# Operand addresses, retention operands one pair at a time, and later weight sums in a four-layer decoder trunk

## The chip, the cores and the metric

The kernel runs as one program on one core of one Trainium2 chip. The metric is device time in microseconds, from launch to end, as the median of three runs. TensorE does the matrix products (its sequencer loads weights and streams a moving operand past them), VectorE (DVE) and ScalarE (ACT) do the elementwise work, GpSimd (POOL) and SyncE (SP) mostly issue DMAs. SBUF is the on-chip memory: 128 partitions, each with one row of bytes in which every tile has a start address. PSUM is where TensorE leaves sums.

## What is computed

Four sub-layers on 512 tokens of width 1024, each with an RMSNorm ahead and a residual add behind: retention, gated FFN, stick-breaking attention, gated FFN; then a last RMSNorm.

```python
for i in range(DEPTH):            # DEPTH = 2
    x = x + _retention(_rmsnorm(x, ret_norm[j]), ...)         # i = 0
    x = x + _stick_breaking(_rmsnorm(x, sb_norm[j]), ...)     # i = 1
    x = x + _conv_ffn(_rmsnorm(x, ffn_norm[i]), ...)          # both
return _rmsnorm(x, final_norm)
# _retention: proj = h @ w_in (q, k, v, g of 4 heads), rotary, chunked decay attention,
#             y = silu(g) * normed o; y @ w_out
# _conv_ffn:  u = h @ w_up; depthwise conv of width 3; (silu(gate) * val) @ w_down
```

All of it is float32. The kernel forms each float32 product from rounded parts: an operand is split into `hi` and `lo`, and a product is hi*hi + hi*lo + lo*hi, three matmuls.

## The kernel before

**Loads.** Every weight chunk goes through `chunk` (L154): SP issues a DMA into a `raw` buffer, ACT casts it to `hi`, DVE subtracts to get `lo` (L159, L160). The buffers are rings of 4 while retention runs and 5 afterwards. A chunk of 1024 columns serves 24 matmuls of 512 columns, or 24 of 256.

**Products.** `mm3` (L163 to L168) and the loops at L357 and L646 issue the three matmuls. In most products the weights are `hi`/`lo` and the moving operand is an activation: `xh`/`xl` (the normed input of a sub-layer), `yy`/`qk` (retention's output), `oh`/`ol` (FFN), `oo` (stick-breaking). For the values of retention and stick-breaking it is the other way: `xh`/`xl` or `xo` are the weights and `hi`/`lo` move.

**Seven products instead of eight.** `seven` (L294) computes a 2x2 block product with seven block products: for retention's heads 2 and 3 (tensors fqk, fv, fg) and for two stages of each FFN's down-projection (fast0_0, fast0_1, fast1_0, fast1_1). It needs sums of weight blocks, which `weight_sums` (L372) makes in DRAM with accumulating DMAs on POOL's queue, in the order of `ORDER`, and sums of operand blocks, which for retention `ret_operands` (L436) makes into `xo` tiles on DVE and ACT, for pairs of k tiles: pairs 0 and 1 in one call, pairs 2 and 3 in another.

**Order in retention** (L516). Head 0; then q, k, v of head 1; operands of pairs 0 and 1; `out_proj(steps, 2)`, half of head 0's output projection (each piece is one weight chunk, 24 matmuls and two adds into `x` at L220); scores, values and gate of head 1; then the pool of the normed input is given back and `xb` takes its place; operands of pairs 2 and 3; the other half of head 0's output projection; all four pieces of head 1's; then heads 2 and 3 by seven products. A planner in the framework may move an instruction ahead of another on its engine where nothing forbids it, so an engine's queue is only roughly in program order. An output projection's sums lie in `acc`, of which there are three.

**Addresses.** SBUF tiles lie on two stacks in every partition's row, and each tile starts at a multiple of 32 bytes. On the left stack stand constants (`vec`, `x`, `ones`, `diag`, ...) up to byte 21,824, which is 64 past a multiple of 256, and then `raw`, `hi`, `lo`, `tt` and the tiles of a phase. All of their sizes, with one exception, are multiples of 256 (the `sg` tiles of stick-breaking are not, but together they take 10,496 bytes, 41 x 256), so every matrix operand there starts 64 past a multiple of 256: `hi`, `lo`, `oh`, `ol`, `yy`, `qk`, `oo` and others. The right stack holds `xh`, `xl`, `xo`, `vx` and grows down from byte 229,344, which is 224 past a multiple of 256; so all of these start 224 past one. A matmul takes slices at multiples of 256 bytes within a tile, which leaves the remainders as they are. The small exceptions are `ones` (160 past) and the identity (0).

Of the kernel before, what the change touches and what calls it, by code (L numbers as in the profile page):

```python
# [9 lines left out]
F32 = mybir.dt.float32  # L10
# [5 lines left out]
P = 128  # L16
D = 1024
S = 512
KD = D // P
# [9 lines left out]
FAST = (2, 2)  # L29
TAIL = 18  # L30
Q = S // 2
HALF = S // 2

ORDER = (
    ("fqk", 0, 1), ("fv", 0, 2), ("fg", 0, 1), ("fqk", 1, 1), ("fg", 1, 1), *((f"fast{l}_{s}", 0, 2) for l in range(2) for s in range(FAST[l])),
)
SUMS = {n for n, _, _ in ORDER}
WARM = 4
RAW = 4
FAST_HEAD = 2  # L40
# [3 lines left out]
class Kernel:  # L44
# [12 lines left out]
    def __init__(self, ctx, tc, t):  # L57
        self.tc, self.nc, self.t = tc, tc.nc, t
        self.const = ctx.enter_context(tc.tile_pool(name="const", bufs=1))
        self.wp = ctx.enter_context(tc.tile_pool(name="wp", bufs=1))  # L60
        self.ap = ctx.enter_context(tc.tile_pool(name="ap", bufs=1))
        self.dp = ctx.enter_context(tc.tile_pool(name="dp", bufs=1, space=bass.MemoryType.DRAM))
        self.ps = ctx.enter_context(tc.tile_pool(name="ps", bufs=1, space=bass.MemoryType.PSUM))
        self.n = 0
        self.pp, self.xpools = None, []
        self.tiles = dict.fromkeys(("raw", "hi", "lo"), 0)
        self.att_pool()
        self.phase("ret")
        self.operands("xa", "xs")
# [130 lines left out]
    def out_proj(self, name, base, ys, last):  # L200
        for _ in self.out_proj_steps(name, base, ys, last):
            pass
# [167 lines left out]
        x, z = ([self.att() for _ in range(2)] for _ in range(2))  # L370
        self.seven(name, i, product, add, x, z, n)

    def weight_sums(self):


        nc, tc, t = self.nc, self.tc, self.t
        self.sums = {n: {} for n in SUMS}
        gate = nc.gpsimd.tensor_copy(self.gate, self.x[KD - 1][:, :1])
        with tc.issue_after(getattr(gate, "ins", gate)):
            for name, first, n in ORDER:  # L380
                w, cs = t[name], range(first, first + n)
                cols = w.shape[3]
                d = {
                    c: [
                        self.dp.tile([P, cols + 16], F32, tag=f"{name}_{c}_{i}", bufs=1, name=self.name("sum"))[:, :cols]
                        for i in range(4)
                    ]
                    for c in cs
                }
                self.sums[name].update(d)  # L390
                s = lambda c, i: d[c][i]
                for to, of in ((0, 2), (2, 0), (0, 3), (2, 2), (1, -1), (1, 0), (3, -2), (3, 1)):
                    for c in cs:
                        if (to, of) in ((0, 3), (2, 2), (1, 0), (3, 1)):
                            nc.gpsimd.dma_start(s(c, to), w[c][of], accum_op=ALU.add)
                        else:
                            nc.gpsimd.dma_start(s(c, to), w[c][of] if of >= 0 else s(c, -1 - of))
# [136 lines left out]
    def retention(self):  # L534
        nc, t = self.nc, self.t
        first = self.first4("rfirst", load=True)
        self.xpl = [self.xa, None]

        def angles(r):
            self.cos, self.sin = self.sb("tr"), self.sb("tr")  # L540
            nc.sync.dma_start(self.cos, t["cos"])
            nc.sync.dma_start(self.sin, t["sin"])
            if r is not None:
                nc.vector.tensor_mul(self.cos, self.cos, r)
                nc.vector.tensor_mul(self.sin, self.sin, r)

        def out_proj(steps, n):
            for _ in range(8 * n):
                next(steps, None)

        def out_steps(h, y, last=None):
            return self.out_proj_steps("rout", 4 * h, y, last)

        angles(self.r)
        nc.sync.dma_start(self.vec[:, 5 * KD :], t["vec"][:, 5 * KD :])
        self.rc = self.token_major_r()
        self.weight_sums()
        self.ops = []
        qk = self.ret_qk(0, first)
        v = self.ret_v(0)  # L560
        y = self.ret_y(0, self.ret_av(v, self.ret_scores(0, *qk)))
        qk = self.ret_qk(1, [])
        v = self.ret_v(1)
        self.ret_operands((0, 1))
        steps = out_steps(0, y)
        out_proj(steps, 2)
        y = self.ret_y(1, self.ret_av(v, self.ret_scores(1, *qk)))

        self.less_operands()
        self.more_operands("xb")  # L570
        self.xpl[1] = self.xp
        angles(None)
        self.ret_operands((2, 3))
        out_proj(steps, 2)
        steps = out_steps(1, y)
        out_proj(steps, 4)
        qk = self.ret_qk(2, self.feature_tiles("fqk", 0))
        v = [[self.sb(tag) for tag in tags] for tags in (("yy",) * NT, ("vr", "vr", "vx", "vx"))]
        self.token_rows("fv", 0, 2, S, v)
        y = self.ret_y(2, self.ret_av(self.ret_split(v[0]), self.ret_scores(2, *qk)))  # L580
        qk = self.ret_qk(3, self.feature_tiles("fqk", 1))
        steps = out_steps(2, y)
        out_proj(steps, 2)
        y = self.ret_y(3, self.ret_av(self.ret_split(v[1]), self.ret_scores(3, *qk)))
        out_proj(steps, 2)
        self.operands("xs")
        for _ in out_steps(3, y, 1):
            pass
# [72 lines left out]
    def ffn(self, l, last):  # L661
        a, s = [], 0
        first = self.first4(f"ufirst{l}")
        self.phase("ffn")
        for f in range(NF):
            a.append(self.ffn_act(l, f, first[2 * f : 2 * f + 2] if f < 2 else (None, None)))
            if f == 1:
                self.swap_pool()
            if s < 2 and f == STAGES[l][s][1] + 1:
                lo, hi = STAGES[l][s]  # L670
                for half in range(2):
                    self.fast_down(l, s, a[lo + 1 : hi : 2], half)
                s += 1
        self.swap_pool()
        self.down(l, a, s, last)
        if last is not None:
            self.phase("sb")
        return a
# [336 lines left out]
```

## Time and profile before

| | |
|---|---|
| median of 3 runs | 1392.52 us (1391.12 to 1393.06) |
| the profiled execution | 1390.32 us |
| its span, first to last instruction | 1388.5 us |
| TensorE busy in it | 1365.5 us, 7280 matmuls |
| VectorE, ScalarE, GpSimd busy | 1038.8, 643.4, 111.0 us |
| chain that ended last, share of TensorE | 88% |
| granted TensorE clock, mean | 0.995 |

The profiled execution has 1.8 us around its span and lies 2.2 us below the median of the runs. A matmul's duration in the profile overlaps that of the next one, so what a matmul costs is the spacing from one start to the next; durations of two groups of the same shape can still be compared.

### The profile page before, as it was taken

The page shows a single profiled execution, that of the slowest core. Times are in us where ns is not written, and L with a number is a line of the kernel's source. Part 1 is how long each engine was busy: PE and PEld are TensorE (multiplying, and loading weights), DVE is VectorE, ACT ScalarE, POOL GpSimd, SP SyncE. Part 2 cuts the span into 40 slices and gives each one's busy share as a digit, 9 for nine tenths or more (in the row PEclk, how much of TensorE's full clock was granted, in tenths as well). Part 3 has the DMA queues.
Part 4 walks back from the last instruction along what each step waited for, and adds up shares of the span by engine and source line. Part 5 has one row for each costly group of instructions (what it writes and reads, how often), then busy time and mean ns, then how long its engine had stood idle before and what let it go on. Part 6 is the DMA issues. An engine that isn't in the chain of part 4 may idle for free.

```text
span 1388.5 us, 18974 instructions
## 1 busy us (share of the span) xinstructions
PE 1365.5 (98%) x7280; PEld 1155.5 (83%) x7280; DVE 1038.8 (75%) x1464; ACT 643.4 (46%) x932; POOL 111.0 (8%) x190
## 2 busy tenths in 40 slices
PE   9999989999999999999999999999999999999997
PEld 7888879789988889888988898787778899888887
DVE  7777667678778878688666668879799886787665
ACT  5544435465645444344334454444265443444434
POOL 1222222120000000000000021111000000000000
PEclk9999999999999999999999999999999999999999
DMA  9999999997334325323521564444143345235121
GB/s 323 292 287 266 277 294 322 318 316 213 113 96 140 106 91 168 121 91 105 181 80 40 170 183 125 129 117 105 44 138 94 104 127 162 75 110 173 54 69 62
DMA packets 68107, 217.98 MB, mean 157 GB/s; under 512 B 8112, under 2 KB 10288, under 8 KB 68016
## 3 DMA queue, kind: packets, MB, share of 16 engines
q1 hardware_dynamic: 45760, 146.21, 32.5%
q0 software_dynamic: 20736, 69.22, 19.9%
q10 hardware_dynamic: 1520, 1.33, 0.3%
q8 instruction: 58, 0.95, 0.3%
q14 instruction: 33, 0.27, 0.1%
HBM read 202.05 MB, written 58.72 MB: 188 GB/s over the span
## 4 chain that ended last, share of the span: by engine, by line
PE 88%; DVE 7%; DMA 3%; ACT 1%; issue 1%; DVEq 0%; ACTq 0%; SPq 0%
PE acc L166 19%; PE acc L168 19%; PE acc L167 19%; PE x L646 6%; PE att L166 4%; PE att L167 4%; PE att L168 4%; PE z L646 3%; PE att L646 3%; PE acc L646 2%; PE one L768 1%; PE z L740 1%; DVE sg L745 1%; PE tp L760 1%; DVE lo L160 1%
## 5 line engine op out<-in xcount | busy, mean ns | idle before, releaser
L159 ACT CAST hi<-raw 128x1024 fp32r<-128x1024 f32 (+2 forms) x255 | 247.4, 971 | 383.9 <-PE acc L167 221.8
L160 DVE TENSOR_TENSOR lo<-raw,hi 128x1024 fp32r<-128x1024 f32 (+2 forms) x255 | 285.6, 1122 | 75.8 <-ACT hi L159 74.6
L167 PE MATMUL acc<-xl,hi 128*128 128x512 f32 x704 | 279.2, 397 | 0.0
L168 PE MATMUL acc<-xh,lo 128*128 128x512 f32 x704 | 279.2, 397 | 0.0
L166 PE MATMUL acc<-xh,hi 128*128 128x512 f32 x704 | 279.1, 396 | 0.0
L168 PEld LDWEIGHTS acc<-xh,lo 128*128 128x128 f32 x704 | 132.6, 188 | 32.1
L167 PEld LDWEIGHTS acc<-xl,hi 128*128 128x128 f32 x704 | 132.6, 188 | 31.1 <-issue 0.2
L166 PEld LDWEIGHTS acc<-xh,hi 128*128 128x128 f32 x704 | 132.6, 188 | 30.8
L601 DVE SCALAR_TENSOR_TENSOR tt<-tt,vec,tt 128x511 f32<-128x511 f32 (+1 forms) x176 | 131.4, 748 | 4.3 <-ACT tt L599 1.7
L598 DVE TENSOR_TENSOR tt<-acc,rr 128x512 f32<-128x512 f32 x80 | 55.1, 689 | 86.3 <-PE acc L168 86.0
L220 DVE TENSOR_TENSOR x<-x,acc 128x512 f32<-128x512 f32 x72 | 48.7, 684 | 40.4 <-PE acc L168 40.1
L599 ACT ACTIVATE tt<-tt,vec 128x512 f32<-128x512 f32 x88 | 71.5, 814 | 10.2 <-DVE tt L598 9.0
L646 PE MATMUL att<-xo,hi 128*128 128x256 f32 x384 | 69.4, 282 | 0.0
L646 PEld LDWEIGHTS att<-xo,hi 128*128 128x128 f32 x384 | 59.2, 189 | 0.2
L745 DVE TENSOR_TENSOR_SCAN sg<-sg,diag 128x512 f32<-128x512 f32 (+3 forms) x64 | 52.4, 819 | 2.4 <-ACT sg L742 1.7
L646 PE MATMUL att<-xo,lo 128*128 128x256 f32 x192 | 53.9, 281 | 0.0
L646 PE MATMUL x<-oh,hi 128*128 128x256 f32 x188 | 53.5, 285 | 0.0
L646 PE MATMUL x<-oh,lo 128*128 128x256 f32 x188 | 53.2, 283 | 0.0
L646 PE MATMUL x<-ol,hi 128*128 128x256 f32 x188 | 53.2, 283 | 0.0
L168 PE MATMUL acc<-hi,xl 128*128 128x256 f32 (+1 forms) x160 | 52.5, 328 | 0.0
L167 PE MATMUL acc<-lo,xh 128*128 128x256 f32 (+1 forms) x160 | 52.3, 327 | 0.0
L166 PE MATMUL acc<-hi,xh 128*128 128x256 f32 (+1 forms) x160 | 52.2, 326 | 0.0
(555 smaller groups left out, 3042.6 us busy)
## 6 DMA issues: line engine op xcount, KB each, us to landing
raw<-in_up SPq DMA_DIRECT2D x80, 512.0 KB, 3.6
raw<-sum SPq DMA_DIRECT2D x48, 512.0 KB, 4.2
sum<-in_fast POOLq DMA_DIRECT2D x36, 512.0 KB, 9.7
sum<-sum POOLq DMA_DIRECT2D x24, 512.0 KB, 7.9
raw<-in_fast SPq DMA_DIRECT2D x18, 512.0 KB, 3.6
raw<-in_rout SPq DMA_DIRECT2D x16, 512.0 KB, 6.1
sk<-hl POOLq DMA_DIRECT2D x32, 256.0 KB, 4.4
sum<-in_fqk POOLq DMA_DIRECT2D x12, 512.0 KB, 9.9
```

Source lines behind the costliest of these rows:

```text
L159: nc.scalar.copy(hi, raw)
L160: nc.vector.tensor_sub(lo, raw, hi.bitcast(F32))
L166: mm(out, a[0], b[0], start=start, stop=False)
L167: mm(out, a[0], b[1], start=False, stop=False)
L168: mm(out, a[1], b[0], start=False, stop=stop)
L220: self.nc.vector.tensor_add(self.x[m], self.x[m], ps)
L598: nc.vector.tensor_mul(u, ps, self.r)
L599: nc.scalar.activation(c, u, AF.Identity, scale=w[2], bias=w[3])
L601: nc.vector.scalar_tensor_tensor(c[:, i:], u[:, : S - i], w[2 - i], c[:, i:], op0=ALU.mult, op1=ALU.add)
L646: mm(out[:, :Q], a[ai], b[bi], start=start and k + i == 0, stop=k == nk - 1 and i == 2, skip_group_check=not start)
L740: nc.tensor.matmul(z[:, :nz], q[:, i * P : (i + 1) * P], k[:, :nz], start=m == 0, stop=m == 1)
L745: nc.vector.tensor_tensor_scan(sg[:, :n][:, ::-1], sg[:, :n][:, ::-1], self.diag[:, S - n :][:, ::-1], 0.0, op0=ALU.mult, op1=ALU.max,)
```

## The change

Three things. Two unused tiles of 192 and 224 bytes are laid at the bottom of the left stack and at the top of the right one, so that left and right operands alike start at multiples of 256 bytes (`ones` then lies 96 past one and the identity 192). Retention's second half of operands is made one pair at a time, with a piece of an output projection ahead, between and behind; for that, one piece of head 0's output projection moves from ahead of head 1's scores to behind its gate, and two of head 1's pieces go ahead of head 0's last two. The sums of the second FFN's weights are issued in a call of their own, in the first FFN, behind a read of that FFN's norm factor `r`; before, they were issued with the others, behind the load of the last `x` tile.

```diff
 ORDER = (
-    ("fqk", 0, 1), ("fv", 0, 2), ("fg", 0, 1), ("fqk", 1, 1), ("fg", 1, 1), *((f"fast{l}_{s}", 0, 2) for l in range(2) for s in range(FAST[l])),
+    (("fqk", 0, 1), ("fv", 0, 2), ("fg", 0, 1), ("fqk", 1, 1), ("fg", 1, 1), ("fast0_0", 0, 2), ("fast0_1", 0, 2)),
+    (("fast1_0", 0, 2), ("fast1_1", 0, 2)),
 )
...
         self.const = ctx.enter_context(tc.tile_pool(name="const", bufs=1))
+
+        self.const.tile([P, 48], F32, name="left")
+        right = ctx.enter_context(tc.tile_pool(name="right", bufs=1, side="right"))
+        right.tile([P, 56], F32, name="right")
...
-    def weight_sums(self):
+    def weight_sums(self, order, behind):
...
-        gate = nc.gpsimd.tensor_copy(self.gate, self.x[KD - 1][:, :1])
+        gate = nc.gpsimd.tensor_copy(self.gate, behind[:, :1])
         with tc.issue_after(getattr(gate, "ins", gate)):
-            for name, first, n in ORDER:
+            for name, first, n in order:
...
-        self.weight_sums()
+        self.sums = {}
+        self.weight_sums(ORDER[0], self.x[KD - 1])
...
         steps = out_steps(0, y)
-        out_proj(steps, 2)
+        out_proj(steps, 1)
         y = self.ret_y(1, self.ret_av(v, self.ret_scores(1, *qk)))
...
-        self.ret_operands((2, 3))
+        out_proj(steps, 1)
+        more = out_steps(1, y)
+        for j in (2, 3):
+            self.ret_operands((j,))
+            out_proj(more, 1)
         out_proj(steps, 2)
-        steps = out_steps(1, y)
-        out_proj(steps, 4)
+        out_proj(more, 2)
...
         first = self.first4(f"ufirst{l}")
+        if l == 0:
+            self.weight_sums(ORDER[1], self.r)
         self.phase("ffn")
```

## Rows read from the trace of the kernel before

**Rows 1.** The page, part 1: busy us (share of the span) xinstructions.
```profile
PE 1365.5 (98%) x7280; PEld 1155.5 (83%) x7280; DVE 1038.8 (75%) x1464; ACT 643.4 (46%) x932; POOL 111.0 (8%) x190
```

**Rows 2.** Waits of TensorE: total us, times, longest us.
```profile
PE acc L166 <- DVE x L220: 4.4, 2, 4.0
PE tp L760 <- DVE bt L749: 2.6, 8, 0.6
PE att L166 <- ACT p L490: 2.1, 1, 2.1
PE att L357 <- DVE vx L368: 1.7, 1, 1.7
```

**Rows 3.** TensorE groups by form: out<-moving,weights (any order) xcount | busy us, mean ns.
```profile
L167 PE MATMUL acc<-xl,hi 128*128 128x512 f32 x704 | 279.2, 397 | 0.0
...
L168 PE MATMUL acc<-hi,xl 128*128 128x512 f32 x64 | 25.5, 399 | 0.0
...
L167 PE MATMUL acc<-lo,xh 128*128 128x512 f32 x64 | 25.2, 394 | 0.0
L166 PE MATMUL acc<-hi,xh 128*128 128x512 f32 x64 | 25.1, 392 | 0.0
...
L168 PE MATMUL acc<-qk,lo 128*128 128x512 f32 x64 | 24.9, 389 | 0.0
...
L646 PE MATMUL att<-xo,lo 128*128 128x256 f32 x192 | 53.9, 281 | 0.0
...
L646 PE MATMUL x<-oh,lo 128*128 128x256 f32 x188 | 53.2, 283 | 0.0
```

**Rows 4.** TensorE's timeline, up-projection, twelve matmuls apart: start us, us.
```profile
449.65 0.40 PE L168 MATMUL acc<-xh,lo 128*128 128x512 f32 x1
...
452.46 0.39 PE L168 MATMUL acc<-xh,lo 128*128 128x512 f32 x1
```

**Rows 5.** TensorE's timeline, retention's output projection, twelve matmuls apart.
```profile
393.67 0.39 PE L166 MATMUL acc<-qk,hi 128*128 128x512 f32 x1
...
396.39 0.39 PE L166 MATMUL acc<-qk,hi 128*128 128x512 f32 x1
```

**Rows 6.** Stretches: us, busy of PE, PEld, DVE, ACT, POOL, granted clock, DMA, GB/s.
```profile
165.00:200.00 35.00, 30.97 (x129) 24.93 (x128) 28.43 (x44) 14.67 (x21) 10.06 (x15) 0.95 1.01 280
260.00:300.00 40.00, 35.60 (x197) 30.82 (x197) 26.58 (x33) 22.96 (x36) 9.55 (x15) 0.96 1.04 324
```

**Rows 7.** VectorE's timeline where operands of pairs 2 and 3 are made.
```profile
176.22 1.41 DVE L455 SCALAR_TENSOR_TENSOR tt<-x,vec,rr 128x512 f32<-128x512 f32 x2
...
182.23 1.41 DVE L455 SCALAR_TENSOR_TENSOR tt<-x,vec,rr 128x512 f32<-128x512 f32 x2
...
187.03 1.88 DVE L220 TENSOR_TENSOR x<-x,acc 128x512 f32<-128x512 f32 x3
```

**Rows 8.** TensorE's timeline just behind its longest wait.
```profile
189.22 0.63 PE L166 MATMUL acc<-yy,hi 128*128 128x512 f32 x1
189.64 0.63 PE L167 MATMUL acc<-yy,hi 128*128 128x512 f32 x1
```

**Rows 9.** The chain of waits, 262 to 290 us: start us, us, what.
```profile
257.45 11.52 DMA raw<-in_fv
...
271.40 8.08 DMA raw<-in_fg
```

**Rows 10.** DMA issues, 245 to 300 us: xcount, KB each, median us to landing.
```profile
raw<-in_fg SPq DMA_DIRECT2D x3, 512.0 KB, 9.8
```

**Rows 11.** DMA issues, 403 to 500 us (first FFN).
```profile
raw<-in_up SPq DMA_DIRECT2D x16, 512.0 KB, 3.6
```

**Rows 12.** POOL's timeline: first and last DMA of the second FFN's sums.
```profile
233.88 0.52 POOL L397 DMA_DIRECT2D sum<-in_fast  x1
...
326.44 0.81 POOL L395 DMA_DIRECT2D sum<-in_fast  x1 [1.95 <-DMA sum<-sum]
```

**Rows 13.** VectorE's timeline: the first FFN's norm factor.
```profile
421.18 3.35 DVE L251 RECIPROCAL rr<-tt 128x512 f32<-128x512 f32 x1 [1.31 <-ACT tt L249]
```

More of the change, by code (lines that the diff above doesn't have):

```diff
@@ L34 @@
 ORDER = (
-    ("fqk", 0, 1), ("fv", 0, 2), ("fg", 0, 1), ("fqk", 1, 1), ("fg", 1, 1), *((f"fast{l}_{s}", 0, 2) for l in range(2) for s in range(FAST[l])),
+    (("fqk", 0, 1), ("fv", 0, 2), ("fg", 0, 1), ("fqk", 1, 1), ("fg", 1, 1), ("fast0_0", 0, 2), ("fast0_1", 0, 2)),
+    (("fast1_0", 0, 2), ("fast1_1", 0, 2)),
 )
-SUMS = {n for n, _, _ in ORDER}
 WARM = 4
@@ L371, in token_rows @@
         self.seven(name, i, product, add, x, z, n)
-    def weight_sums(self):
+    def weight_sums(self, order, behind):
         nc, tc, t = self.nc, self.tc, self.t
-        self.sums = {n: {} for n in SUMS}
-        gate = nc.gpsimd.tensor_copy(self.gate, self.x[KD - 1][:, :1])
+        gate = nc.gpsimd.tensor_copy(self.gate, behind[:, :1])
         with tc.issue_after(getattr(gate, "ins", gate)):
-            for name, first, n in ORDER:
+            for name, first, n in order:
                 w, cs = t[name], range(first, first + n)
@@ L389, in weight_sums @@
                 }
-                self.sums[name].update(d)
+                self.sums.setdefault(name, {}).update(d)
                 s = lambda c, i: d[c][i]
```

## The prediction

> **What bounds the kernel now.** I read the page's busy times first, then TensorE's waits, then its groups by form, then short pieces of its timeline. TensorE is busy in 98% of the span [rows 1], and its waits add up to some 12 us, of which three of the four largest lie in retention [rows 2]. So there are two places where time can come from: the few stalls, and the pace of 7280 matmuls. The pace is not the same for equal shapes. With 512 columns, twelve matmuls whose moving operand is xh or xl take 452.46 - 449.65 = 2.81 us, 234.2 ns each [rows 4]; twelve whose moving operand is qk take 396.39 - 393.67 = 2.72 us, 226.7 ns each [rows 5]. The durations say the same over all of them: 397 against 389 ns [rows 3]. Line, weights (hi and lo), shape and output are alike; what differs is the place of the moving operand, 224 past a multiple of 256 bytes for xh and xl, 64 past one for qk, and the weights at 64 in both.
>
> **Part 1, addresses.** After the change both operands start at remainder 0. No matmul at full pace has that now, so its cost has to be bounded. The nearest row is the one in which moving operand and weights have the same remainder, 64 and 64 [rows 5]; I take it, since equal remainders are kept by the change and 64 and 0 differ by a power of two above 32, while 224 is an odd multiple of 32. Then:
> - Moving xh or xl, 512 columns. By the code: up-projections 80 chunks x 24, head 1's q and k 4 x 24, two heads' gates 8 x 24, stick-breaking's q and k 12 x 24, four first stages of 96, and 96 at the end of stick-breaking's output projection: 1920 + 96 + 192 + 288 + 384 + 96 = 2976. Of these, 2592 stand in long rows of their like: 2592 x 7.5 ns = 19.4 us. The 384 in stick-breaking are broken up by small float32 matmuls; I give them half, 1.4 us.
> - Weights xh, xl or xo, moving hi or lo, 512 columns: two heads' values, 2 x 96, and seven products x 24 for heads 2 and 3, 360 in all. They have 392, 394 and 399 ns, mean 395, against 389 [rows 3]: 360 x 6 ns = 2.2 us.
> - Moving xo, 256 columns: 4 calls x 168 = 672. Here 281 ns at 224 stands against 283 at 64 [rows 3], so this part loses 672 x 2 ns = 1.3 us.
> - The rest has 64 and 64 already: nothing.
>
> Sum: 19.4 + 1.4 + 2.2 - 1.3 = 21.7 us off. It all lies on TensorE, which sets the end. VectorE (75%) and ScalarE (46%) [rows 1] have room for a pace 1.6% higher; where VectorE already ends last, in stick-breaking's transposes (2.6 us in eight waits [rows 2]), a faster fill uncovers at most what was gained there, 1.4 us.
>
> The bounds are far apart. Above: the slowest group without a wait is 399 ns [rows 3], 10 ns over qk's. Below: 512 columns at 2.4 GHz are 213.3 ns, 13.4 less than qk's spacing; and at the 1.2 GHz level, behind the long stall, matmuls follow each other in 0.42 us [rows 8], which is 512 columns at 1.2 GHz with nothing on top. So what is on top at full clock isn't in the matmul itself, and better addresses might take more of it away. Both ends are rivals below.
>
> A rule speaks against this part. The Trainium skill (TensorE: Matmul & The Clock Gate, What happens when you issue a matmul) gives TensorE two independent read ports into SBUF, one for the moving operand and one for the weights; and SBUF — State Buffer (Specifications (TRN2)) has lines of 16 bytes, of which 64, 224 and 0 are all multiples. By these the address would do nothing, and the sum below would lose its 21.7 us; the 7.5 ns between the two timelines speak against that here.
>
> **Part 2, retention's operands.** VectorE makes both pairs in one stretch, from 176.22 to 187.03 us, 5 to 6 us for each pair, and three adds into x wait behind it [rows 7]. TensorE has filled its three sums by then and stands for 4.0 us [rows 2]. It then runs at the lower clock for a while (0.95 over 35 us, 1.7 us of work [rows 6]). After the change VectorE's longest stretch between two adds is one pair, under 6 us; three sums last TensorE 3 x 12 x 0.227 = 8.2 us. A piece is 5.4 us of TensorE's time and, with a pair, some 8.4 us of VectorE's (pair 5.6, two adds 1.4, one lo 1.2), so VectorE falls behind by 3 us in each of the two pieces; the piece ahead gives it two free microseconds and the three sums take up the rest. I take the whole stall: -4.2 (with the refill) -1.7 = -5.9 us; the bound on the other side is that a stall of 3 us stays. The piece taken from ahead of head 1's scores covered nothing that lacks cover: VectorE and ScalarE wait for TensorE there. Its load moves with it on SP's queue; two pieces of head 1 going ahead cost nothing, since the last part of its y is split some 4 us behind its gate and one piece, 5.4 us, stands between.
>
> **Part 3, later sums.** The second FFN's sums run from 233.88 to 326.44 us on POOL's queue [rows 12]. In that time loads need 9.8 us [rows 10] instead of 3.6 in the first FFN [rows 11], and the chain of waits goes through two of them, 11.52 and 8.08 us, both followed by a cast and a subtraction [rows 9]; there TensorE waits 1.7 and 2.1 us [rows 2], and 0.04 x 40 = 1.6 us go with the clock [rows 6]. Without the sums these loads would land 4 to 6 us sooner, more than either wait. With the short matmuls around them I count 5.5 us off. The sums then start behind the first FFN's norm factor, at 421.18 + 3.35 = 424.5 us [rows 13], and last some 93 us again [rows 12]. Queued behind the gate on POOL is nothing that the first FFN needs. Loads there become slower, to perhaps 8 to 10 us; but the five buffers hold more than 20 us of work at 24 x 0.227 = 5.4 us a chunk, and the same sums beside the same kind of loads stalled nothing from 20 to 180 us. I take 0; if the cover failed, it would cost what it costs now, up to 6 us. The sums end near 518 us, before or just as the faster consumption of the down-projection begins.
>
> **Sum.** -21.7 - 5.9 - 5.5 = -33.1 us on the profiled execution: 1390.3 - 33.1 = 1357.2. It lies 2.2 us under the median of its runs, so the forecast is 1359 us.
>
> **Rivals.**
> - Addresses do more: remainder 0 is better than 64 and part of the 13.4 ns above the bare columns goes on nearly all of some 6900 split matmuls. All of it would be 92 us; half of it gives 1359 - 46 = 1313. For it: the bare pace at the lower clock [rows 8]. Against: qk and oh, whose operands agree, have just this rest.
> - Addresses do nothing, and 397 against 389 has its cause in another property of xh and xl, such as their height in the row: only the stalls go, 1392.5 - 11.4 = 1381. Against: yy, qk and oh, written by the same engines as xh, are at 389, and as weights xh is slow too [rows 3]. The two pages of the Trainium skill named above would give this outcome.
> - The sums stall the first FFN instead: 1359 + 6 = 1365. For: loads of 10 us beside them [rows 10]. Against: the depth of the ring.
> - Slower: operands and weights that all start at multiples of 256 meet in one part of the memory, and every long stream takes the slowest unstalled duration, 399 ns, and the 256-column ones 2 ns more [rows 3]. That is 2 ns x 2976 + 10 ns x some 750 + 4 x 360 + 2 ns x 2800 = 20.5 us, which eats the 11.4 us of the stalls: 1392.5 + 20.5 - 11.4 = 1402. It decides from an average loss of 11.4 us / 6900 = 1.7 ns a matmul. Against: equal remainders are the best case now.
>
> **How the numbers follow.** Forecast 0.60 (its own range 1349 to 1369), sums stall 0.08, addresses do nothing 0.10, more 0.15, slower 0.07. The range takes the first three whole (0.78) and the near edge of the fourth, down to 3.5 ns more a matmul: 1335 to 1384. About 0.2%, 2.8 us, is what a measurement of this kernel can tell from no change: faster 0.93, within 0.01, slower 0.06.
>
> **What would show it.** Right: xh's groups at 389 ns and its spacing at 226.7, xo's at 283; the wait for L220 gone, the clock at 1.00 in both stretches; loads of 4 to 5 us near 260 us; no wait for a cast between 424 and 520 us. Wrong: 397 ns kept (addresses do nothing), spacings under 224 ns (more), oh or qk above 389 (slower), a new wait of TensorE behind L220 near 190 us or behind L159 in the first FFN.

## The result, and the profile after

| | before | changed kernel |
|---|---|---|
| median | 1392.79 us (1391.12 to 1393.58, 4 runs) | 1355.58 us (1355.27 to 1356.42, 4 runs) |
| ratio, 95% interval | | 0.9735 (0.9718 to 0.9752) |
| profiled execution | 1390.32 us | 1356.42 us |
| span | 1388.5 us | 1354.6 us |

The change takes 37.2 us off the median and 33.9 us off the profiled execution; the forecast was 1359, with 33.1 us between profiled executions. The changed kernel's busy times (part 1 of its page) answer to [rows 1]: TensorE has 26.5 us less, the others do the same work.

```profile
PE 1339.0 (99%) x7280; PEld 1152.2 (85%) x7280; DVE 1035.6 (76%) x1464; ACT 644.1 (48%) x932; POOL 111.7 (8%) x191
```

Its groups by form answer to [rows 3] (line, engine, operation, out<-operands, shape, xcount | busy us, mean ns):

```profile
L172 PE MATMUL acc<-xl,hi 128*128 128x512 f32 x704 | 274.6, 390 | 0.0
L654 PE MATMUL att<-xo,lo 128*128 128x256 f32 x192 | 54.3, 283 | 0.0
L654 PE MATMUL x<-oh,lo 128*128 128x256 f32 x188 | 53.2, 283 | 0.0
...
L173 PE MATMUL acc<-hi,xl 128*128 128x512 f32 x64 | 24.9, 389 | 0.0
L173 PE MATMUL acc<-qk,lo 128*128 128x512 f32 x64 | 24.9, 389 | 0.0
```

The groups of split matmuls that stand in long rows of their like are at 389 to 390 ns with 512 columns and at 282 to 284 with 256. The up-projection's timeline, twelve matmuls apart, answers to [rows 4]: 444.40 - 441.68 = 2.72 us, 226.7 ns each.

```profile
441.68 0.39 PE L171 MATMUL acc<-xh,hi 128*128 128x512 f32 x1
...
444.40 0.39 PE L171 MATMUL acc<-xh,hi 128*128 128x512 f32 x1
```

TensorE's waits (total us, times, longest) answer to [rows 2]. The waits behind L220 and for vx are gone; one for `p` stands there again, but in another place (below).

```profile
PE tp L770 <- DVE bt L759: 2.8, 8, 0.6
PE one L288 <- DVE diag L284: 1.6, 1, 1.6
PE att L171 <- ACT p L494: 1.5, 1, 1.5
PE att L171 <- ACT hi+_1263_6881 L164: 1.0, 1, 1.0
```

Three stretches (us, busy of PE, PEld, DVE, ACT, POOL, granted clock, DMA share, GB/s), the first two answering to [rows 6]. TensorE works through all of them at full clock, the last one, with the second FFN's sums beside it, included.

```profile
161.00:196.00 35.00, 35.00 (x156) 29.00 (x155) 28.93 (x46) 14.42 (x20) 8.22 (x13) 1.00 1.01 296
253.00:293.00 40.00, 40.00 (x263) 37.08 (x262) 31.57 (x43) 26.24 (x39) 0.00 (x0) 1.00 0.47 150
400.00:500.00 100.00, 100.00 (x443) 82.76 (x442) 84.70 (x104) 50.73 (x57) 22.69 (x33) 1.00 0.93 263
```

Loads (KB each, median us to landing) from 240 to 295 us, against [rows 10], and then in the first FFN, against [rows 11]: the late loads have moved with the sums.

```profile
raw<-in_fg SPq DMA_DIRECT2D x3, 512.0 KB, 4.8
```

```profile
raw<-in_up SPq DMA_DIRECT2D x11, 512.0 KB, 7.8
```

VectorE's timeline where the second half of the operands is made, against [rows 7]: adds into x (L225) now stand between and within the pairs, the longest distance between two being 3.1 us.

```profile
173.88 0.68 DVE L225 TENSOR_TENSOR x<-x,acc 128x512 f32<-128x512 f32 x1
174.48 1.62 DVE L469 TENSOR_TENSOR xo<-tt,xo 128x512 fp32r<-128x512 f32 x3
...
176.68 0.68 DVE L225 TENSOR_TENSOR x<-x,acc 128x512 f32<-128x512 f32 x1
...
179.08 0.69 DVE L225 TENSOR_TENSOR x<-x,acc 128x512 f32<-128x512 f32 x1
...
180.02 2.23 DVE L469 TENSOR_TENSOR xo<-tt,xo 128x512 fp32r<-128x512 f32 x4
182.16 0.68 DVE L225 TENSOR_TENSOR x<-x,acc 128x512 f32<-128x512 f32 x1
```

The wait that is new lies where the moved piece was. A load lands late and is cast at 134.41 us (ACT); its subtraction (L165) stands ahead of the scores (L492) on VectorE, and TensorE, which has done the scores, waits for them until 138.03. First ACT, then VectorE, then TensorE:

```profile
134.41 1.05 ACT L164 CAST hi<-raw 128x1024 fp32r<-128x1024 f32 x1 [5.25 <-DMA raw<-in_rg]
...
137.36 1.34 ACT L494 CAST p<-tt 128x512 fp32r<-128x512 f32 x3 [1.89 <-DVE tt L492]
```

```profile
135.50 1.23 DVE L165 TENSOR_TENSOR lo<-raw,hi 128x1024 fp32r<-128x1024 f32 x1 [1.84 <-ACT hi L164]
136.64 1.48 DVE L492 TENSOR_TENSOR tt<-att,dc 128x512 f32<-128x512 f32 x3
```

```profile
138.03 0.97 PE L171 MATMUL att<-p,vv 128*128 128x512 f32 x3 [1.52 <-ACT p L494]
```

### The profile page after: what moved, and what is told of

Same layout as the page of the kernel before. It is cut to its first block, busy times and chain, and to the rows that moved or that the text cites. A ratio compares the mean times of both kernels' runs of the same rounds, so it can differ in the third digit from the quotient of the medians.

```text
span 1354.6 us, 18982 instructions
## 1 busy us (share of the span) xinstructions
PE 1339.0 (99%) x7280; PEld 1152.2 (85%) x7280; DVE 1035.6 (76%) x1464; ACT 644.1 (48%) x932; POOL 111.7 (8%) x191
## 4 chain that ended last, share of the span: by engine, by line
PE 94%; DVE 4%; issue 1%; ACT 1%; DMA 1%; DVEq 0%; ACTq 0%
PE acc L171 20%; PE acc L172 20%; PE acc L173 20%; PE x L654 6%; PE att L654 5%; PE att L171 4%; PE att L172 4%; PE att L173 4%; PE z L654 3%; PE acc L654 2%; PE att L362 2%; PE one L778 1%; PE z L750 1%; DVE sg L755 1%; PE tp L770 1%; DVE at L772 1%
## 5 line engine op out<-in xcount | busy, mean ns | idle before, releaser
L165 DVE TENSOR_TENSOR lo<-raw,hi 128x1024 fp32r<-128x1024 f32 (+2 forms) x255 | 285.3, 1121 | 64.4 <-ACT hi L164 63.1
L172 PE MATMUL acc<-xl,hi 128*128 128x512 f32 x704 | 274.6, 390 | 0.0
L171 PE MATMUL acc<-xh,hi 128*128 128x512 f32 x704 | 274.3, 390 | 0.0
L173 PE MATMUL acc<-xh,lo 128*128 128x512 f32 x704 | 274.2, 390 | 0.0
L172 PEld LDWEIGHTS acc<-xl,hi 128*128 128x128 f32 x704 | 132.2, 188 | 26.5 <-issue 0.2
L225 DVE TENSOR_TENSOR x<-x,acc 128x512 f32<-128x512 f32 x72 | 48.9, 685 | 35.0 <-PE acc L173 34.9
L616 ACT ACTIVATE tt<-tt 128x512 f32<-128x512 f32 x44 | 27.8, 631 | 53.7 <-DVE tt L609 53.6
```

The costliest lines, as they stand in the source:

```text
L165: nc.vector.tensor_sub(lo, raw, hi.bitcast(F32))
L171: mm(out, a[0], b[0], start=start, stop=False)
L172: mm(out, a[0], b[1], start=False, stop=False)
L173: mm(out, a[1], b[0], start=False, stop=stop)
L225: self.nc.vector.tensor_add(self.x[m], self.x[m], ps)
L616: nc.scalar.activation(g, g, AF.Silu)
```

## The experiments

### One part at a time

**Addresses alone.** The kernel before with the two unused tiles.

```diff
+        self.const.tile([P, 48], F32, name="left")
+        right = ctx.enter_context(tc.tile_pool(name="right", bufs=1, side="right"))
+        right.tile([P, 56], F32, name="right")
```

> The kernel before with only the two unused tiles: all operands at multiples of 256 bytes, order of work and of the sums as before. My theory (the pace of a 512-column matmul depends on where its operands start): the groups that move xh and xl go from 397 to 389-390 ns, their spacing from 234 to 226.7 ns, and the time falls by 21.7 us to about 1371 us; the stalls near 183 us (4.2 us) and near 267 and 279 us (1.8 and 2.3 us) stay, each within 1 us. Rival (the pace gain is eaten by VectorE, which gets no faster): the spacing falls but the waits of TensorE for VectorE grow by more than 3 us in all, and the time stays above 1375 us.

1371.32 us against 1392.98, ratio 0.9845 (0.9832 to 0.9857): 21.7 us off, the term of the sum. xl's group is at 390 ns here too, and in the up-projection's timeline twelve matmuls take 449.83 - 447.11 = 2.72 us, 226.7 ns each:

```profile
447.11 0.39 PE L169 MATMUL acc<-xh,hi 128*128 128x512 f32 x1
...
449.83 0.39 PE L169 MATMUL acc<-xh,hi 128*128 128x512 f32 x1
```

TensorE's waits:

```profile
PE acc L169 <- DVE x L223: 6.5, 2, 4.0
PE tp L763 <- DVE bt L752: 2.7, 8, 0.6
PE att L169 <- ACT p L493: 2.4, 1, 2.4
...
PE att L169 <- ACT vr L369: 1.3, 1, 1.3
```

The long wait behind the adds is still 4.0 us; what has grown in its line is another one, near 340 us, from 0.3 to 2.5 us. Between 220 and 300 us TensorE waits 4.8 us instead of 4.4, but not in the same places: that for vx is down to 0.5 us, further than the 1 us expected, with 1.3 us for vr in its stead. TensorE's waits for VectorE add up to 11.9 us against 10.9, less than the 3 us that the rival named; all of its waits to 16.6 us against 14.0. A faster TensorE uncovers a little of what VectorE and the loads do, where the sums run beside them.

**Operands alone.** The kernel before with the new order in retention.

```diff
-        out_proj(steps, 2)
+        out_proj(steps, 1)
         y = self.ret_y(1, ...)
...
+        out_proj(steps, 1)
+        more = out_steps(1, y)
+        for j in (2, 3):
+            self.ret_operands((j,))
+            out_proj(more, 1)
```

> The kernel before with only the new order in retention (operands one pair at a time, one piece of head 0's output projection moved behind the gate). My theory: the 4.2 us stall near 183 us and the stretch at the lower clock behind it go (-5.9 us), and the wait of head 1's values for their scores that stands in the changed kernel near 136 us (1.7 us) appears: 1392.8 - 5.9 + 1.7 = 1388.6 us. Rival (the stall only moves, since VectorE's work in this stretch is the same): a wait of 2 us or more behind L220 between 165 and 220 us, and a time within 1.5 us of before.

1386.86 us (1382.73 to 1389.55), ratio 0.9955 (0.994 to 0.9969): some 6 us off, within 4 to 8. From 160 to 195 us TensorE has no idle time and full clock, so the stall didn't move to that place. The wait near 136 us that was expected isn't there: TensorE has none from 120 to 160 us in this trace (why is told with the moved piece, below). Where the loads are late TensorE is idle for 4.7 us instead of 4.4 and the clock is at 0.91 instead of 0.96 [rows 6], and the runs lie further apart than any other kernel's:

```profile
160.00:195.00 35.00, 35.00 (x155) 28.74 (x154) 30.50 (x48) 15.03 (x22) 7.88 (x12) 1.00 0.98 274
260.00:300.00 40.00, 35.28 (x215) 31.80 (x214) 24.47 (x32) 21.57 (x35) 10.04 (x15) 0.91 1.02 300
```

**Later sums alone.**

```diff
-        self.weight_sums()
+        self.weight_sums(ORDER[0], self.x[KD - 1])
...
+        if l == 0:
+            self.weight_sums(ORDER[1], self.r)
```

> The kernel before with only the second FFN's sums moved into the first FFN. My theory: the two waits near 267 and 279 us and the lower clock behind them go (-5.5 to -6.3 us), nothing comes in the first FFN, though its loads get slower (8 us in place of 3.6): about 1387 us. Rival (those waits come from the order on VectorE and ScalarE, not from late loads): both waits stay within 0.5 us and the time is within 1 us of before. Second rival: waits for casts between 424 and 525 us give the gain back.

1382.28 us, ratio 0.9925 (0.9913 to 0.9937): 10.7 us off, twice the term of the sum and some 5 us under the time expected; between the profiled executions it is 8.3 us. The stretch of the two waits, and the first FFN with the sums in it:

```profile
260.00:300.00 40.00, 40.00 (x258) 36.55 (x257) 29.15 (x38) 24.21 (x37) 0.00 (x0) 1.00 0.40 124
420.00:520.00 100.00, 100.00 (x462) 81.94 (x461) 85.96 (x113) 48.93 (x56) 19.69 (x28) 1.00 0.88 248
```

Both waits are gone with the sums and nothing else changed; the loads of fg land in 4.2 us instead of 9.8 [rows 10]. So late loads were their cause; and nothing is given back. The first rival and the second fall.

The three parts add up to 21.7 + 6.1 + 10.7 = 38.5 us; together they gave 37.2.

### What in an address counts

The forecast took remainder 0 to be as good as 64 because the two operands agree in both, and also because both are multiples of 64. Five placements tell the two reasons apart.

**Both at 64.**

```diff
-        self.const.tile([P, 48], F32, name="left")
-        right.tile([P, 56], F32, name="right")
+        right.tile([P, 40], F32, name="right")
```

> The changed kernel without the left tile and with 160 bytes on the right, so that all matrix operands start 64 past a multiple of 256. If operands have to agree in their remainder, or have to be multiples of 64: spacing 226.7 ns and the changed kernel's time, 1355 to 1357 us. If multiples of 128 or 256 are what counts: a spacing over 228 ns and more than 1362 us.

1355.37 us (1354.77 to 1356.37): the changed kernel's time, xl's group at 390 ns. Multiples of 256, or of 128, aren't needed.

**Both at 32.**

```diff
-        self.const.tile([P, 48], F32, name="left")
+        self.const.tile([P, 56], F32, name="left")
-        right.tile([P, 56], F32, name="right")
+        right.tile([P, 48], F32, name="right")
```

> The changed kernel with 224 bytes on the left and 192 on the right: all matrix operands 32 past a multiple of 256, so they agree, but are no multiples of 64. If agreement is what counts: 226.7 and 120.0 ns, 1355 to 1357 us. If multiples of 64 count: over 230 ns for 512 columns also where qk and oh move, which were at 226.7 before, and 1375 us or more.

1355.40 us (1354.67 to 1356.49), and the same durations:

```profile
L172 PE MATMUL acc<-xl,hi 128*128 128x512 f32 x704 | 274.6, 390 | 0.0
L654 PE MATMUL att<-xo,lo 128*128 128x256 f32 x192 | 54.3, 283 | 0.0
```

Multiples of 64 aren't needed either; agreement is enough.

**Left at 0, right at 64.**

```diff
-        right.tile([P, 56], F32, name="right")
+        right.tile([P, 40], F32, name="right")
```

> The changed kernel with 160 bytes on the right instead of 224: weights and left operands at multiples of 256, xh, xl and xo 64 past one. If each operand has only to be a multiple of 64: spacing 226.7 ns for matmuls that move xh, and 1355 to 1357 us. If the two have to agree in their remainder: 230 to 238 ns, and about 1375 us.

1364.64 us, ratio 0.9804 (0.9786 to 0.9823): between the two expectations, 9.1 us over the changed kernel.

```profile
L172 PE MATMUL acc<-xl,hi 128*128 128x512 f32 x704 | 277.2, 394 | 0.0
L654 PE MATMUL att<-xo,lo 128*128 128x256 f32 x192 | 53.6, 279 | 0.0
...
L171 PE MATMUL acc<-hi,xh 128*128 128x256 f32 x96 | 26.6, 277 | 0.0
```

Here xl is slow although both operands are multiples of 64. It is not slow to the same degree everywhere: in the first FFN's up-projection the spacing is 228.9 ns on the mean up to 640 us and 233.3 from there on, and 233.3 in the second FFN, with tiles at the same remainders throughout. That is why the time lies between the expectations. Two pieces of the timeline, twelve matmuls apart each, 2.75 and 2.80 us:

```profile
620.07 0.39 PE L171 MATMUL acc<-xh,hi 128*128 128x512 f32 x1
...
622.82 0.39 PE L171 MATMUL acc<-xh,hi 128*128 128x512 f32 x1
```

```profile
689.66 0.40 PE L171 MATMUL acc<-xh,hi 128*128 128x512 f32 x1
...
692.46 0.40 PE L171 MATMUL acc<-xh,hi 128*128 128x512 f32 x1
```

And the groups of 256 columns are *faster* than where the operands agree: 277 to 279 ns against 283.

**Left at 0, right at 32**, and **left at 0, right at 128**: the same line with 48 and with 24 columns.

> The changed kernel with 192 bytes on the right: left at 0, right at 32 past a multiple of 256. Both theories (agreement, multiples of 64) expect the slow pace of before for xh and xl, about 234 ns, and 1355.6 + 21.7 = 1377 us; if only the distance between 224 and 64 was bad, the pace is 226.7 ns and the time 1356 us.

> The changed kernel with 96 bytes on the right: left at 0, right at 128 past a multiple of 256, the one distance in steps of 64 that no run has had. If agreement modulo 128 is enough: 226.7 ns for matmuls that move xh, and 1355 to 1357 us. If it has to be modulo 256: 230 to 235 ns and 1364 to 1377 us.

1375.14 us (0.9877, 0.9859 to 0.9895) and 1372.68 us (0.9854, 0.9837 to 0.987). First right at 32, then right at 128:

```profile
L172 PE MATMUL acc<-xl,hi 128*128 128x512 f32 x704 | 278.4, 395 | 0.0
```

```profile
L172 PE MATMUL acc<-xl,hi 128*128 128x512 f32 x704 | 277.9, 395 | 0.0
```

Agreement modulo 128 isn't enough. The table has the spacing for each distance of the moving operand from its weights, modulo 256: the mean from one start to the next over all neighbours of one shape and placement in a trace (357 to 4062 of them at 512 columns, 371 to 2563 at 256), gaps over 1.25 times the median left out.

| moving minus weights | run | 512 columns, ns | 256 columns, ns |
|---|---|---|---|
| 0 | changed kernel; both at 64; both at 32 | 227.2 | 119.9 |
| 32 | left 0, right 32 (xh, xo move) | 233.4 | 117.2 |
| 64 | left 0, right 64 (xh, xo move) | 230.9 | 117.8 |
| 96 | before (hi, lo move) | 233.3 | 119.9 |
| 128 | left 0, right 128 (xh, xo move) | 232.6 | 119.6 |
| 160 | before (xh, xo move) | 234.2 | 118.4 |
| 192 | left 0, right 64 (hi, lo move) | 233.3 | 114.6 |
| 224 | left 0, right 32 (hi, lo move) | 233.3 | 118.3 |

In long rows at distance 0 the spacing is the same from matmul to matmul, 226 or 227 ns; elsewhere it runs through a pattern, 231 to 238 ns in the up-projection of the kernel before. Rows with xh and xo moving and rows with hi and lo moving are different loops, so only the whole table, not each step in it, speaks of the distance alone: with 256 columns the loop that moves hi and lo has 119.5 ns at distance 0, so that 119.9 at 96 is no gain there. Nor does the distance always fix the spacing, as the 228.9 and 233.3 ns at 64 show, of which 230.9 is a mix. And all weights of a loop lie at one remainder, while the next matmul's weights are loaded beside the one that runs (PEld is busy in 85% of the span, PE in 99%): the runs can't tell which of the two the moving operand has to agree with.

### Using it

**oh and ol at 192.** The shape of 256 columns was faster at most distances other than 0; the FFN's down-projection is nearly all of it.

```diff
         self.phase("ffn")
+        self.ph.tile([P, 48], F32, name=self.name("skew"))
...
             if f == 1:
+                self.ph.tile([P, 16], F32, name=self.name("unskew"))
```

> The changed kernel with the FFN's oh and ol tiles moved up by 192 bytes (two unused tiles of 192 and 64 bytes in the FFN's pool), so that they start 192 past a multiple of 256 and their weights at 0; all else as in the changed kernel. In the run with left 0 and right 64 the 256-column matmuls whose moving operand was 64 behind its weights came every 114.6 ns, against 120.0 where both agree, and the 512-column ones every 233.3 against 226.7. If the distance of moving operand to weights (modulo 256) sets the pace, whatever the tiles: 1452 matmuls of 256 columns gain 5.4 ns (7.8 us), 240 of 512 columns lose 6.6 ns (1.6 us), and the time is 1355.6 - 6.2 = 1349.4 us. If the 114.6 ns belonged to that place alone (stick-breaking, with other matmuls between): 120 ns as before, and 1355 to 1357 us.

1351.02 us (1350.11 to 1352.41), ratio 0.9701 (0.9687 to 0.9716): faster than both kernels, by less than expected.

```profile
L654 PE MATMUL x<-oh,lo 128*128 128x256 f32 x188 | 52.6, 280 | 0.0
...
L173 PE MATMUL acc<-oh,lo 128*128 128x512 f32 x70 | 27.5, 395 | 0.0
```

oh's 256-column spacing is 116.3 ns, not 114.6, and its 512-column one 233.3, as expected: 1446 x 3.6 - 238 x 6.6 ns = 3.6 us. The median is 4.6 us under the changed kernel's; about 1.2 us of it is the wait for `p`, 0.3 us in this trace instead of 1.5. So the distance acts on another tile and in another loop too, but 116.3 is a mean of several patterns: part of oh's matmuls came every 113.3 ns and part every 117.8, at the same remainders (the run with both, below, has two pieces of the timeline). Which pattern comes when stays open.

**The moved piece kept ahead.** Two orders that have both of head 0's first pieces ahead of head 1's scores again.

```diff
-        out_proj(steps, 1)
+        out_proj(steps, 2)
         y = self.ret_y(1, ...)
...
         out_proj(steps, 1)
+        self.ret_operands((2,))
+        out_proj(steps, 1)
         more = out_steps(1, y)
-        for j in (2, 3):
-            self.ret_operands((j,))
-            out_proj(more, 1)
-        out_proj(steps, 2)
-        out_proj(more, 2)
+        self.ret_operands((3,))
+        out_proj(more, 4)
```

> The changed kernel, with both pieces of head 0's output projection ahead of head 1's scores as before, and behind the gate: piece, operands of pair 2, piece, operands of pair 3, then the four pieces of head 1. My theory (the moved piece was the cover of a late load whose subtraction stands ahead of the scores on VectorE): the 1.5 us wait near 136 us goes and nothing comes, about 1354 us. Rival (with all of head 1's pieces behind the operands the wait behind L220 comes back): a wait of 1 us or more near 170 to 190 us, and 1355 us or more.

1354.24 us (1353.81 to 1354.92), with no wait for `p`. In this order both pairs are taken from x after head 0's third and fourth pieces have been added to their tiles, so it computes with other values of x; the work is the same, and its time is that of the order. The next one keeps every operand ahead of the adds to its tiles:

```diff
-        out_proj(steps, 1)
+        out_proj(steps, 2)
         y = self.ret_y(1, ...)
...
-        out_proj(steps, 1)
         more = out_steps(1, y)
-        for j in (2, 3):
-            self.ret_operands((j,))
-            out_proj(more, 1)
-        out_proj(steps, 2)
-        out_proj(more, 2)
+        self.ret_operands((2,))
+        out_proj(steps, 1)
+        out_proj(more, 1)
+        self.ret_operands((3,))
+        out_proj(steps, 1)
+        out_proj(more, 3)
```

> The changed kernel with both of head 0's first pieces ahead of head 1's scores, as in the kernel before, and behind the gate: operands of pair 2, one piece of head 0, one of head 1, operands of pair 3, one piece of head 0, three of head 1. My theory (the moved piece was the cover of a late load): no wait near 136 us in the profile, and 1354 to 1355 us. Rival (a pair with no piece ahead of it brings the wait behind L220 back): such a wait of 1 us or more between 165 and 195 us, and 1355.5 us or more.

1354.17 us (1353.96 to 1354.47), ratio 0.9723 (0.9709 to 0.9738), TensorE's waits:

```profile
PE tp L770 <- DVE bt L759: 2.7, 8, 0.6
...
PE att L171 <- ACT hi+_1263_6881 L164: 1.0, 1, 1.0
```

No wait for `p`, none behind the adds: theory held, rival not. The intervals of the two ratios, this kernel's and the changed one's, overlap, though; and of the 2.2 us between their profiled executions 1.1 come within the first hundred matmuls, ahead of anything that differs. Nor is the wait the same in all programs that have the changed kernel's order. It hangs on when one load lands. Where ScalarE stands for that load ahead of its cast for 4.07, 4.14, 5.07, 5.25 and 6.32 us (oh and ol at 192, both at 64, right at 32, the changed kernel, right at 128), TensorE waits for `p` 0.3, 0.4, 1.3, 1.5 and 2.6 us; where the cast stands for TensorE instead (operands alone, both at 32, right at 64), there is no such wait. None of the six programs with both pieces ahead of the scores has it.

**Both.** The changed kernel with oh and ol at 192 and with that last order, the edits of the two put together.

> The order of the run with the pair first together with oh and ol 192 past a multiple of 256. The two act in different places, so their gains against the changed kernel should add: 1355.6 - 4.6 - 1.4 = 1349.6 us, with no wait near 136 us and 116 to 117 ns for oh's 256-column matmuls. Rival: the wait near 136 us was in part of the executions only and its gain was chance, 1351 us.

1350.93 us (1350.59 to 1353.12), ratio 0.9707 (0.9694 to 0.972). The gains didn't add. oh and ol at 192 alone has only 0.3 us of that wait in its profile, so there was next to nothing left to take; the rival's reading, that this wait comes in some executions, fits better than mine. And oh's matmuls lost a little: their spacing is 116.8 ns on the mean, not 116.3, which is 0.7 us over 1446 of them. The same matmuls in the same stretch of the first FFN run in one pattern with oh and ol at 192 alone and in another here, at the same remainders: twelve take 531.38 - 530.02 = 1.36 us there, 113.3 ns each, and 531.17 - 529.76 = 1.41 us here, 117.5 ns each.

```profile
530.02 0.28 PE L654 MATMUL x<-oh,hi+_975_5077 128*128 128x256 f32 x1
...
531.38 0.28 PE L654 MATMUL x<-oh,hi+_975_5077 128*128 128x256 f32 x1
```

```profile
529.76 0.28 PE L654 MATMUL x<-oh,hi+_975_5077 128*128 128x256 f32 x1
...
531.17 0.28 PE L654 MATMUL x<-oh,hi+_975_5077 128*128 128x256 f32 x1
```

## Why the prediction held, step by step

**Part 1, addresses (-21.7 us): right in size; half of its reason fell.** Addresses alone gave 21.7 us. The spacing taken from [rows 5] is the one measured, and xo's small loss (281 to 283 ns) came too. That the medians agree with the sum to the tenth has luck in it: between the profiled executions it is 18.1 us. Matmul by matmul, addresses alone are 4.5 us ahead of before at the 1200th, 0.1 at the 1950th and 17.8 at the end: the pace gives some 22 us, and 4.4 of it are lost to longer waits in and behind the stretch in which the sums run. But "64 and 0 differ by a power of two above 32, while 224 is an odd multiple of 32" had nothing to do with it: both at 32 is as fast as both at 0, and 64 against 0 is slow. The other reason, equal remainders, is what the runs bear out. By the rule of the Trainium skill (TensorE: Matmul & The Clock Gate, What happens when you issue a matmul) the two read ports are independent, which taken alone would make the placement free; by the measurements it isn't: the long rows of the up-projection went from 234.2 to 226.7 ns with nothing but two tiles added.

**Part 2, operands (-5.9 us): the stall went, the piece's cover was missed.** In the changed kernel the starts of the matmuls around the stall gain 5.9 us on those of before between the 800th matmul and the 850th. VectorE's blocks came out shorter than I had argued, since the planner put adds inside a pair as well. The step that failed is "covered nothing that lacks cover": the moved piece was the time in which a load landed and was subtracted ahead of head 1's scores. That cost 1.5 us in the profiled execution, and from nothing to 2.6 us in others of the same order.

**Part 3, later sums (-5.5 us): right in mechanism, too small.** Between the 1200th and the 1300th matmul the changed kernel gains 7.2 us, and the kernel with the later sums alone 6.9. I had counted the two waits and the clock, 5.4 us, and 0.1 for the short gaps around them; TensorE's idle time in that stretch is 40.00 - 35.60 = 4.4 us [rows 6], which with the clock makes 6.0; where the other 0.9 of the 6.9 lie, these rows don't tell. Medians give 10.7 us for this part alone. What is beyond the trace may come from executions of before that wait longer than the profiled one, which lay 2.2 us below its median: with the sums in retention the runs of a kernel spread over 2 to 7 us (addresses alone, operands alone), without them over 0.5 to 3.3 us (1.2 in later sums alone and the changed kernel, 3.3 with left at 0 and right at 64). The two ranges overlap and no profile of a longer execution of before was taken, so this is argued and not shown. The forecast lay 3.4 us above the result, though it was 0.8 us off between the profiled executions: I had carried the 2.2 us over to the changed kernel, whose profiled execution was 0.8 us above its median, not below it.

**The cover in the first FFN held.** Loads there take 7.8 us instead of 3.6, and TensorE waits for none of them from 400 to 500 us.

**Readings that were off.** TensorE's waits add up to 14.0 us, not to some 12. The groups of yy were at 397 to 405 ns before, not 389, since the matmuls at the lower clock behind the long wait [rows 8] are among them; in the changed kernel they are at 389. And "the rest has 64 and 64 already" leaves out stick-breaking's values, 384 matmuls of 256 columns with xh and xl (224) as weights; they were at 281 to 282 ns and are at 282 to 283. None of the three moves the sum by more than 0.2 us.

**The rivals.** That addresses do nothing falls by 390 against 397 ns; that they do more, by a spacing that is still 226.7 and not less at remainder 0; that operands at equal remainders are slow, by the same rows; that the sums stall the first FFN, by a stretch without idle time. My reading of [rows 8] as room for more at full clock found some, but only for 256 columns, and in the other direction: by operands that do not agree.

## What to carry to other kernels

Where TensorE is the bound, compare the spacing of matmuls of the same shape over different tiles: a steady difference of 3% is worth more than most stalls, and here it went by placing two tiles of 192 and 224 bytes. Try the distance between moving operand and weights for each shape by itself, as the best one for 512 columns was not the best for 256, and measure it in more than one place, as at a distance of 64 the pace was not the same in all places. Before work is moved off the front of a dependent step, ask which late load it was covering, and move bulk transfers out of stretches whose loads land late into ones whose buffers run far ahead.

## What the runs showed that was not expected

- Whether a matmul's two operands agree modulo 256 counts, not the remainder of either: 0, 32 and 64 alike on both sides give 227.2 ns at 512 columns, each of seven other distances 230.9 to 234.2 ns.
- Where they don't agree, the distance doesn't always fix the pace: at a distance of 64 the same loop ran at 228.9 and at 233.3 ns, and at 192 the same matmuls at 113.3 ns in one program and 117.8 in another.
- At 256 columns agreement isn't the best: 119.5 to 120.0 ns there, down to 114.6 ns at a distance of 192 and 116.3 ns with other tiles at that distance; at 96 and 128 there was next to no gain (119.9 and 119.6).
- Beside the sums' transfers a 512 KB load took 9.8 us to land in retention and 7.8 in the first FFN (medians), without them 4.8 and 3.6 us.
